# Eleven pairs of projection stripes by seven half-size products instead of eight, and a recurrence taken block by block

## The chip, the cores and the metric

The kernel runs on one core of a Trainium2 chip. The metric is the device time of one launch in microseconds (us); lower is better.

## The reference

One layer of a decoder trunk in fp32, for a prompt of 1024 tokens and 8 single new tokens (1032 columns in all, NT). A normalised input is multiplied by one wide weight; its columns are cut into u and z (recurrent branch and its gate path), q, k, v of 24 heads, za (the gate path of the attention) and two sets of merge gates, g:

```python
D_IN = 2 * D_RNN + 3 * N_GROUPS * D_ATTN + D_ATTN + 2 * D_MODEL      # 9216 columns, D_MODEL = 1024 rows
xn = rms_norm(x, norm_pre);  u, z, q, k, v, za, g_a, g_r = split(xn @ w_in)
xc = causal_conv(u, ...)                          # 4 taps, per channel
r, i = sigmoid(block_diag(xc, w_a) + b_a), sigmoid(block_diag(xc, w_x) + b_x)
a = exp(-8 r softplus(-lam));  b = sqrt(1 - a*a) * i * xc;   h[t] = a[t] h[t-1] + b[t]
y_rnn = (h * silu(z)) @ w_rnn_out
y_att = (merge of three dilated attentions * silu(za)) @ w_attn_out
y = x + rms_norm((sigmoid(g_a) * y_att + sigmoid(g_r) * y_rnn) @ w_out)
```

The new k and v rows, the last convolution inputs and the last h are outputs too.

## The kernel before, in words

Activations lie transposed: 128 channels on the partitions, the 1032 columns (tokens) along the free axis. Eight tiles of the normalised input, each as two fp32r parts (`xh`, `xl`), stay in SBUF as the moving operand. An fp32 product is three fp32r matmuls (`mm3`: hi*hi, hi*lo, lo*hi). A **stripe** is 128 output columns of `w_in`: its 512 KB of weights are loaded by SP, split into `whi` (ACT, L236) and `wlo` (DVE, L237, two instructions of 128x512 each), and multiplied chunk by chunk of the 1032 columns, 8 k-tiles of 3 matmuls each into one PSUM bank. `CHUNKS` cuts the columns into 256, 384 and 392; `EARLY` into 256, 256, 256 and 264. So a stripe is 72 matmuls, or 96 with `EARLY`.

There are 72 stripes. Four (`FIRST`, with `EARLY`) run while the input is still being normalised, up to 72.4 us of the trace. Then come 23 (`EARLY_BLOCKS`: z, u, gates g, za), each evacuated from PSUM as it is made: u by ACT into an `ext` tile, z and za by a sigmoid on ACT and a product on DVE (L563), gates by a sigmoid on ACT (L1131) and a write to DRAM. Beside them runs the recurrence, `chain(j)`, two blocks of 128 channels at a time: convolution on DVE (L587 to L592), splits (L601), 12 small gate matmuls on PE, products on POOL (L619, L649, L659), factors on DVE (L643 to L647) and the scan (L653). The last `chain` falls into the next stage: 36 stripes of q, k and v with the attention beside them. Then come 9 late gate stripes, and from 1065 us the output products.

The program is one stream of matmuls in order. A counter, `clk`, is advanced by `mm`; every other piece of work is a generator in a lane (`spawn`), or a call put off by `later`, and `tick` lets it emit its instructions when `clk` has passed the delay that it yielded. Those delays (`yield 4000` and so on) and the place of `W.work()`, which emits a weight split ahead of its use, set the order of each engine's queue, and each engine then takes its queue strictly in order. Tiles come from an arena of 45 slots of [128 x 1040] fp32 (`new`, `ar.free`).

## Time and profile before

| | us |
|---|---|
| median of 3 runs (1265.29 to 1268.86) | 1267.33 |
| the profiled execution | 1264.49 |
| its span | 1262.7 |
| PE busy in it | 1242.1 |
| DVE, ACT, POOL busy | 607.2, 558.1, 217.3 |

The profiled execution lies 2.84 us under the median, and its span 1.8 us under its own time. Busy time is an engine's time in instructions; a wait in its queue isn't counted.

### The profile page before, as it was taken

How to read it: one execution, taken by the hardware profiler on the slowest of the kernel's cores; microseconds unless marked ns; L12 is line 12 of the kernel's file. 1: busy time of each engine (PE TensorE's matmuls, PEld its weight loads, DVE VectorE, ACT ScalarE, POOL GpSimd, SP SyncE). 2: the span in 40 equal slices, each digit the busy share in tenths (PEclk: the TensorE clock that was granted, in tenths of full speed). 3: DMA queues.
4: the chain of work that ended last, by engine and by line, in shares of the span. 5: the costliest groups of instructions: out<-in, count | busy, mean ns of one | idle time of the engine just before them, and what ended most of it. 6: DMA issues, size and time to landing. Idle time of an engine off the chain costs nothing.

```text
span 1262.7 us, 21509 instructions
## 1 busy us (share of the span) xinstructions
PE 1242.1 (98%) x8701; PEld 1197.0 (95%) x8701; DVE 607.2 (48%) x1319; ACT 558.1 (44%) x1236; POOL 217.3 (17%) x232
## 2 busy tenths in 40 slices
PE   9999999999999999999999999999999999999997
PEld 8999999999988999999998999899999999999997
DVE  6562471582764453644256234644254335554226
ACT  7636646547449844334434344344462322223222
POOL 5000320221300221340026001430027000002001
PEclk9999999999999999999999999999999999999999
DMA  8121223132220144722093124712095375313015
GB/s 258 34 84 51 68 84 89 29 101 67 79 73 5 51 122 102 187 68 50 19 233 90 34 68 116 186 55 68 9 260 152 127 256 168 106 51 118 19 51 201
DMA packets 169929, 125.98 MB, mean 100 GB/s; under 512 B 36009, under 2 KB 155785, under 8 KB 169822
## 3 DMA queue, kind: packets, MB, share of 16 engines
q1 hardware_dynamic: 169830, 124.61, 34.0%
q8 instruction: 68, 1.11, 0.4%
q14 instruction: 31, 0.25, 0.1%
HBM read 98.44 MB, written 26.21 MB: 99 GB/s over the span
## 4 chain that ended last, share of the span: by engine, by line
PE 60%; issue 6%; DVE 3%; ACT 1%; DMA 1%; POOL 1%; SPq 0%; DVEq 0%; ACTq 0%; POOLq 0%
PE ps_pj L157 41%; PE ps_pt L157 10%; PE ps_s L157 3%; PE ps_o L157 3%; PE ps_pt L161 2%; PE ps_s L161 1%; DVE ck L1079 1%; DMA sgd<-sg 1%; DVE wlo L237 1%; POOL uc L619 0%; DVE P L841 0%; ACT P L845 0%; SPq L957 0%; ACT L1131 0%; POOL ck L1076 0%
## 5 line engine op out<-in xcount | busy, mean ns | idle before, releaser
L157 PE MATMUL ps_pj<-xh,whi 128*128 128x256 f32 (+2 forms) x1400 | 457.3, 327 | 2.7 <-DVE vt L736 1.4
L157 PE MATMUL ps_pj<-xh,wlo 128*128 128x256 f32 (+2 forms) x1400 | 445.0, 318 | 0.3 <-DVE wlo L250 0.3
L157 PE MATMUL ps_pj<-xl,whi 128*128 128x256 f32 (+2 forms) x1400 | 445.0, 318 | 0.0
L237 DVE TENSOR_TENSOR wlo<-wraw,whi 128x512 fp32r<-128x512 f32 x176 | 147.2, 839 | 337.6 <-ACT whi L236 326.6
L157 PEld LDWEIGHTS ps_pj<-xh,whi 128*128 128x128 f32 x1400 | 263.2, 188 | 12.2 <-issue 8.2
L157 PEld LDWEIGHTS ps_pj<-xh,wlo 128*128 128x128 f32 x1400 | 263.2, 188 | 0.5 <-DVE wlo L250 0.5
L157 PEld LDWEIGHTS ps_pj<-xl,whi 128*128 128x128 f32 x1400 | 263.4, 188 | 0.1
L845 ACT ACTIVATE P<-P,stat 128x128 f32<-128x128 f32 (+1 forms) x192 | 84.3, 440 | 66.6 <-DVE stat L841 66.6
L157 PE MATMUL ps_pt<-xh,whi 128*128 128x256 f32 (+3 forms) x360 | 112.9, 314 | 0.0
L157 PE MATMUL ps_pt<-xl,whi 128*128 128x256 f32 (+3 forms) x360 | 112.4, 312 | 0.0
L157 PE MATMUL ps_pt<-xh,wlo 128*128 128x256 f32 (+3 forms) x360 | 112.2, 312 | 0.0
L236 ACT ACTIVATE whi<-wraw 128x512 fp32r<-128x512 f32 x176 | 109.7, 625 | 3.7 <-DVE hzl L1264 3.0
L157 PEld LDWEIGHTS ps_pt<-xl,whi 128*128 128x128 f32 x360 | 67.7, 188 | 0.1
L157 PEld LDWEIGHTS ps_pt<-xh,whi 128*128 128x128 f32 x360 | 67.7, 188 | 0.0
L157 PEld LDWEIGHTS ps_pt<-xh,wlo 128*128 128x128 f32 x360 | 67.7, 188 | 0.0
L728 ACT ACTIVATE qt<-ps_pj,qsc 128x384 f32<-128x384 f32 (+1 forms) x36 | 27.6, 767 | 75.7 <-PE ps_pj L157 74.0
L841 DVE CUSTOM_DVE_ANT_0 P<-ps_s,base 128x128 f32<-128x128 f32 (+1 forms) x192 | 56.0, 347 | 7.7 <-PE ps_s L157 6.9
L614 ACT ACTIVATE gate<-ps_s,par 64x256 f32<-64x256 f32 (+2 forms) x96 | 52.1, 543 | 16.9 <-PE ps_s L157 15.6
L862 ACT ACTIVATE PT<-ps_pt 128x256 f32<-128x256 f32 (+1 forms) x48 | 20.9, 435 | 68.0 <-PE ps_pt L161 67.9
L619 POOL TENSOR_TENSOR uc<-uc,gate 128x1032 f32<-128x1032 f32 x8 | 20.2, 2536 | 173.7 <-ACT gate L614 173.7
L732 ACT ACTIVATE kt<-ps_pj 128x384 f32<-128x384 f32 (+1 forms) x36 | 24.4, 677 | 52.0 <-PE ps_pj L157 52.0
L1028 POOL TENSOR_TENSOR ck<-ck,qb 128x1024 f32<-128x1024 f32 x12 | 29.4, 2448 | 104.0 <-DMA ck<-in_cache_kv_w 49.9
(284 smaller groups left out, 2122.8 us busy)
## 6 DMA issues: line engine op xcount, KB each, us to landing
wraw<-in_w_in SPq DMA_DIRECT2D x72, 512.0 KB
ck<-in_cache_kv_w SPq DMA_DIRECT2D x24, 512.0 KB
sgd<-sg SPq DMA_DIRECT2D x16, 516.0 KB
sgl<-sgd SPq DMA_DIRECT2D x16, 516.0 KB
xin<-in_x_prompt SPq DMA_DIRECT2D x16, 512.0 KB
qb<-sd SPq DMA_DIRECT2D x12, 512.0 KB
fb<-fd SPq DMA_DIRECT2D x24, 256.0 KB
hzd<-uc SPq DMA_DIRECT2D x8, 516.0 KB
```

The costliest lines, as they stand in the source:

```text
L157: nc.tensor.matmul(out, lhsT, rhs, start=start, stop=stop)
L161: nc.tensor.transpose(out, in_, idn)
L236: nc.scalar.activation(hi[:, a:b], raw[:, a:b], AF.Copy)
L237: nc.vector.tensor_tensor(lo[:, a:b], raw[:, a:b], f32(hi[:, a:b]), op=OP.subtract)
L614: nc.scalar.activation(G[gate][rows, cs], p[at:at + 64, :n], AF.Sigmoid, bias=par[rows, b, 5 + gate:6 + gate])
L619: nc.gpsimd.tensor_tensor(x, x, gi, op=OP.mult)
L728: nc.scalar.activation(dst, src, AF.Copy, scale=C["qsc"][:, g, hp:hp + 1])
L732: nc.scalar.activation(dst, src, AF.Copy)
L841: nc.vector.tensor_tensor_reduce(out=pt[:, h, :128 * n], in0=ps[h][:, off:off + 128 * n], in1=base, scale=-SLOPES[g][2 * hp + h] * DIL[g], ...
L845: nc.scalar.activation(pt[:, h, :128 * n], pt[:, h, :128 * n], AF.Exp, scale=-1.0, bias=st[:, g, 0, h, b:b + 1], accum_out=st[:, g, 1, h, ...
L862: nc.scalar.activation(t, src, AF.Copy)
L1028: nc.gpsimd.tensor_tensor(kc, kc, qb, op=OP.mult)
```

## The change

The first stage now makes six single stripes (`FIRST` gains z0 and z1). The other 22 stripes ahead of the attention are taken as 11 **pairs** of 256 columns. Weight (8 k-tiles by 2 stripes) and input (8 k-tiles by 1032 columns) are each cut into four quarters, and the four quarters of the output come from seven products of sums of quarters (`STEPS`) where plain blocks take eight. One product is 4 k-tiles, 128 columns of weight and half of the columns (520, in chunks of 256 and 264): 24 matmuls, so a pair has 168.

- Input: the tiles are now kept as two halves of 520 columns with both parts, `X[h, k]`. `make_sums` builds the sums s1, s2 and s4 (three POOL and seven DVE operations for each of four k, three of ACT), `make_s3` builds s3 (one POOL, three DVE, one ACT). The quarter x21 is given up after that, kept in DRAM (`xd`) and split anew by `x21_back` while the last pair runs.
- Weights: `pair_pieces` makes three sums and one more on POOL (L295 to L301), and seven splits (ACT L286, DVE L287), at most `OPS` = 4 operands alive.
- Outputs: DVE adds the products from PSUM into quarters (`add`, L636, 14 a pair) and ACT copies the first (2 a pair). u, z, za and g go to DRAM (`leave`).
- Recurrence: `lru(b)` takes one block at a time in five reserved slots, reads u and z back from DRAM and makes z's silu itself (ACT, and one more product on POOL, L902). It runs beside the pairs and the attention. The silu of za moved into the merge behind the attention.
- All single stripes now use `EARLY`; there are 6 + 36 + 8 of them. The PSUM banks are given out by stage (`MODES`).

```diff
-LATE_GATES = 9
-FIRST = [("u", 0), ("u", 1), ("g", 0), ("g", 1)]
-EARLY_BLOCKS = [("z", 0), ("z", 1), ("u", 2), ("u", 3), ("g", 2), ("g", 3),
-                ("z", 2), ("z", 3), ("u", 4), ("u", 5), ("g", 4), ("g", 5),
-                ("z", 4), ("z", 5), ("u", 6), ("u", 7), ("g", 6), ("a", 0),
-                ("z", 6), ("z", 7), ("a", 1), ("a", 2), ("a", 3)]
+LATE_GATES = 8
+FIRST = [("u", 0), ("u", 1), ("g", 0), ("g", 1), ("z", 0), ("z", 1)]
+PAIRS = [("u", 2), ("g", 2), ("z", 2), ("u", 4), ("g", 4), ("z", 4), ("u", 6), ("g", 6), ("z", 6), ("a", 0), ("a", 2)]
...
+        def pair_pieces(self, i):
+            r0, r1 = self.raw[i]
...
+                self.live += 1
+                return t
+            def split(name, src):
+                t = op(name)
+                nc.scalar.activation(t[:, 0], src, AF.Copy)
+                nc.vector.tensor_tensor(t[:, 1], src, f32(t[:, 0]), op=OP.subtract)
...
+            def first():
+                split("b11", b11)
+                t.append(new([128, 2, 4, 128], F32, "wsum"))
+                t1, t2 = t[0][:, 0], t[0][:, 1]
+                nc.gpsimd.tensor_tensor(t1, b12, b11, op=OP.subtract)
+                nc.gpsimd.tensor_tensor(t2, b22, t1, op=OP.subtract)
+                nc.gpsimd.tensor_tensor(b12, b22, b12, op=OP.subtract)
+            def second():
+                split("t2", t[0][:, 1])
+                nc.gpsimd.tensor_tensor(t[0][:, 1], b21, t[0][:, 1], op=OP.subtract)
+            def third():
+                split("t3", b12)
+                ar.free(r0)
+            def sixth():
+                split("t4", t[0][:, 1])
+                ar.free(t[0])
```

```diff
+    def make_sums():
+        for k in range(4):
+            x11, x12, x21, x22 = X[0, k], X[0, k + 4], X[1, k], X[1, k + 4]
+            s1, s2, s4 = (SX.setdefault((q, k), new([128, 2, HALF], F32R, q)) for q in ("s1", "s2", "s4"))
+            ta, tb = (new([128, 2, HALF], F32, "xsum") for _ in range(2))
+            nc.gpsimd.tensor_tensor(ta[:, 0], f32(x21[:, 0]), f32(x21[:, 1]), op=OP.add)
+            nc.vector.tensor_tensor(ta[:, 1], f32(x22[:, 0]), f32(x22[:, 1]), op=OP.add)
+            nc.sync.dma_start(xd[k], ta[:, 0])
+            nc.gpsimd.tensor_tensor(tb[:, 1], f32(x12[:, 0]), f32(x12[:, 1]), op=OP.add)
+            nc.vector.tensor_tensor(tb[:, 0], f32(x11[:, 0]), f32(x11[:, 1]), op=OP.add)
+            yield 1200
+            nc.gpsimd.tensor_tensor(ta[:, 1], ta[:, 0], ta[:, 1], op=OP.add)
+            nc.vector.tensor_tensor(tb[:, 0], ta[:, 1], tb[:, 0], op=OP.subtract)
+            nc.vector.tensor_tensor(tb[:, 1], tb[:, 1], tb[:, 0], op=OP.subtract)
+            yield 1200
+            both = ((s1, ta[:, 1]), (s2, tb[:, 0]), (s4, tb[:, 1]))
+            for t, src in both:
+                nc.scalar.activation(t[:, 0], src, AF.Copy)
+            yield 1000
+            for t, src in both:
+                nc.vector.tensor_tensor(t[:, 1], src, f32(t[:, 0]), op=OP.subtract)
+            ar.free(ta, tb)
+            yield 1200
...
+    def make_s3():
+        for k in range(4):
+            while len(ar.slots) < 3:
+                yield 500
+            x11, x21 = X[0, k], X.pop((1, k))
+            t = new([128, 2, HALF], F32, "xsum")
+            s3 = SX["s3", k] = new([128, 2, HALF], F32R, "s3")
+            nc.gpsimd.tensor_tensor(t[:, 0], f32(x21[:, 0]), f32(x21[:, 1]), op=OP.add)
+            nc.vector.tensor_tensor(t[:, 1], f32(x11[:, 0]), f32(x11[:, 1]), op=OP.add)
+            ar.free(x21)
+            yield 600
+            nc.vector.tensor_tensor(t[:, 1], t[:, 1], t[:, 0], op=OP.subtract)
+            nc.scalar.activation(s3[:, 0], t[:, 1], AF.Copy)
+            nc.vector.tensor_tensor(s3[:, 1], t[:, 1], f32(s3[:, 0]), op=OP.subtract)
+            ar.free(t)
```

```diff
+    def x21_back():
+        for k in range(0, 4, 2):
+            while len(ar.slots) < 4:
+                yield 500
+            t = new([128, 2, HALF], F32, "xsum")
+            nc.sync.dma_start(t, xd[k:k + 2].rearrange("k p c -> p k c"))
+            yield 3500
+            for q in range(2):
+                x = X[1, k + q] = new([128, 2, HALF], F32R, "x1b")
+                nc.scalar.activation(x[:, 0], t[:, q], AF.Copy)
+                nc.vector.tensor_tensor(x[:, 1], t[:, q], f32(x[:, 0]), op=OP.subtract)
+            ar.free(t)
...
+    STEPS = (("b11", "x11"), ("t2", "s2"), ("t3", "s3"), ("t1", "s1"), ("b21", "x12"), ("t4", "x22"), ("b22", "s4"))
...
+    def project_pair(close, last=False):
+        i = W.use_pair()
+        p1 = [small.tile([128, 264], F32, tag="t1", name="p1") for _ in range(2)]
+        for step, (wname, xname) in enumerate(STEPS):
+            w = W.op(i, wname)
+            if step == 1:
+                tb = new([128, 2, HALF], F32, "qb")
+            if step == 3:
+                ta = new([128, 2, HALF], F32, "qa")
+            for c, (o, n) in enumerate(((0, 256), (256, 264))):
+                p = ps_tile("c")[:, :n]
+                for k in range(4):
+                    x = x_op(xname, k)
+                    mm3(p, w[:, 0, k], w[:, 1, k], x[:, 0, o:o + n], x[:, 1, o:o + n], k == 0, k == 3)
+                    if k == 1:
+                        W.work()
+                        yield None
+                cs = slice(o, o + n)
+                q1, q2 = tb[:, 0, cs] if step else None, tb[:, 1, cs] if step else None
+                add = lambda to, by: nc.vector.tensor_tensor(to, p, by, op=OP.add)
+                if step == 0:
+                    nc.scalar.activation(p1[c][:, :n], p, AF.Copy)
+                elif step == 1:
+                    add(q2, p1[c][:, :n])
+                elif step == 2:
+                    add(q1, q2)
+                elif step == 3:
+                    add(q2, q2)
+                    add(ta[:, 1, cs], q1)
+                elif step == 4:
+                    add(ta[:, 0, cs], p1[c][:, :n])
+                elif step == 5:
+                    add(q1, q1)
+                else:
+                    add(q2, q2)
+                yield None
+            W.drop(i, wname)
...
+                    ar.free(SX.pop(("s1", k)))
+                spawn("sums", x21_back())
```

```diff
+    def lru(b):
...
+        L = room["L"]
+        e, r, x = L(0, [128, EXT]), L(1, [128, CV]), L(2, [128, NT])
...
+        s, z = L(0, [128, NT]), L(1, [128, NT])
+        nc.sync.dma_start(z, zd[b])
...
+        nc.scalar.activation(a, z, AF.Sigmoid)
+        yield 3500
+        nc.gpsimd.tensor_tensor(z, z, a, op=OP.mult)
+        nc.gpsimd.tensor_tensor(x, x, z, op=OP.mult)
```

```diff
     for e in started:
         advance(e)
+    spawn("sums", make_sums())
+    for what, i in FIRST[4:]:
+        advance(proj_uz(what, i))
+    until(lambda: "sums" not in lanes)
+    mode[0] = "pair"
+    spawn("sums", make_s3())
     clear_low_w()
-    C = late_consts()
...
+    def lru_start():
+        while "sums" in lanes or len(ar.slots) < 7:
+            yield 500
+        room["L"] = Room(ar, 5)
+    spawn("lru", lru_start())
+    for b in range(KB):
+        spawn("lru", lru(b))
...
+    for q, (what, i) in enumerate(PAIRS):
+        advance(project_pair(pair_of(what, i), last=q == len(PAIRS) - 1))
```

**Ahead of the first pair, DVE and POOL.** DVE before, from the first weight split (of the fifth stripe) after the four first stripes; `cv`, `uc` and `low_w` are the recurrence's, `zs` the silu of z:

```order
L237 TENSOR_TENSOR wlo_1087<-wraw_381,whi_1086 128x512
L582 TENSOR_TENSOR low_w_135<-lrw_850,lh 64x128 x2
L587 SCALAR_TENSOR_TENSOR cv_1110<-ext_269,par,cv_1110 128x1056
L588 SCALAR_TENSOR_TENSOR cv_1110<-ext_269,par,cv_1110 128x1056
L563 TENSOR_TENSOR zs_1085<-ps_pt,zs_1085 128x256
L237 TENSOR_TENSOR wlo_1087<-wraw_381,whi_1086 128x512
L563 TENSOR_TENSOR zs_1085<-ps_pj,zs_1085 128x384
```

DVE of the change from the split of z1's weights; `x` are input tiles, `xsum` the plain sums, `s` the sums' parts:

```order
L268 TENSOR_TENSOR wlo_972<-wraw_390,whi_971 128x512
L560 TENSOR_TENSOR xsum_995<-x_4_29_128 128x520
L563 TENSOR_TENSOR xsum_996<-x_0_17_116 128x520
L566 TENSOR_TENSOR xsum_996<-xsum_995,xsum_996 128x520
L567 TENSOR_TENSOR xsum_996<-xsum_996 128x520
L268 TENSOR_TENSOR wlo_972<-wraw_390,whi_971 128x512
L574 TENSOR_TENSOR s_64_992<-xsum_995,s_64_992 128x520
L574 TENSOR_TENSOR s_65_993<-xsum_996,s_65_993 128x520
L574 TENSOR_TENSOR s_66_994<-xsum_996,s_66_994 128x520
L560 TENSOR_TENSOR xsum_1069<-x_5_30_129 128x520
L563 TENSOR_TENSOR xsum_1070<-x_1_18_117 128x520
```

POOL of the change at the same place; the program before has no such sums:

```order
L559 TENSOR_TENSOR xsum_995<-x_0_25_124 128x520
L562 TENSOR_TENSOR xsum_996<-x_4_21_120 128x520
L565 TENSOR_TENSOR xsum_995<-xsum_995 128x520
L559 TENSOR_TENSOR xsum_1069<-x_1_26_125 128x520
L562 TENSOR_TENSOR xsum_1070<-x_5_22_121 128x520
L565 TENSOR_TENSOR xsum_1069<-xsum_1069 128x520
L295 TENSOR_TENSOR wsum_1145<-wraw_421 128x512
```

DVE goes on in that manner to the last part of s3, L592. From the first row shown to that one it has 49 rows; 47 of them take two tiles from SBUF, and two take one of theirs from PSUM. POOL has 20 sums up to there, and two clears of `low_w`. In the old program POOL's next sum of two tiles comes only with L619.

**A pair, DVE and POOL.** DVE before, in the recurrence's second half:

```order
L643 SCALAR_TENSOR_TENSOR gate_1369<-gate_1368,gate_1369 128x1032
L645 TENSOR_SCALAR gate_1368<-gate_1369 128x1032
L237 TENSOR_TENSOR wlo_1737<-wraw_1536,whi_1736 128x512
L647 SCALAR_TENSOR_TENSOR sq_1690<-gate_1368,sq_1690 128x1032
L563 TENSOR_TENSOR zs_1735<-ps_pj,zs_1735 128x256
L643 SCALAR_TENSOR_TENSOR gate_1389<-gate_1388,gate_1389 128x1032
L237 TENSOR_TENSOR wlo_1737<-wraw_1536,whi_1736 128x512
L645 TENSOR_SCALAR gate_1388<-gate_1389 128x1032
L563 TENSOR_TENSOR zs_1735<-ps_pt,zs_1735 128x384
L647 SCALAR_TENSOR_TENSOR sq_1692<-gate_1388,sq_1692 128x1032
L563 TENSOR_TENSOR zs_1735<-ps_pt,zs_1735 128x392
```

DVE of the change, in the fourth pair; `wop` are a pair's weight operands, `qa` and `qb` the quarters, `room` the recurrence's tiles:

```order
L287 TENSOR_TENSOR wop_2487<-wraw_2241,wop_2487 128x512
L636 TENSOR_TENSOR qb_2271<-ps_c,qb_2271 128x256
L636 TENSOR_TENSOR qb_2271<-ps_c,qb_2271 128x264
L287 TENSOR_TENSOR wop_2528<-wsum_2438,wop_2528 128x512
L287 TENSOR_TENSOR wop_2566<-wraw_2242,wop_2566 128x512
L636 TENSOR_TENSOR qb_2558<-ps_c,p_2515 128x256
L888 SCALAR_TENSOR_TENSOR room_2310<-room_2309,room_2310 128x1032
L636 TENSOR_TENSOR qb_2558<-ps_c,p_2516 128x264
L890 TENSOR_SCALAR room_2310<-room_2310 128x1032
L287 TENSOR_TENSOR wop_2599<-wsum_2438,wop_2599 128x512
L636 TENSOR_TENSOR qb_2558<-ps_c,qb_2558 128x256
L892 SCALAR_TENSOR_TENSOR room_2491<-room_2310,room_2491 128x1032
```

POOL of the change at that place:

```order
L295 TENSOR_TENSOR wsum_2438<-wraw_2241 128x512
L296 TENSOR_TENSOR wsum_2438<-wraw_2242,wsum_2438 128x512
L297 TENSOR_TENSOR wraw_2241<-wraw_2242,wraw_2241 128x4x128
L808 COPY us<-qa_2346 128x8
L301 TENSOR_TENSOR wsum_2438<-wraw_2242,wsum_2438 128x512
L878 TENSOR_TENSOR room_2132<-room_2132,room_2310 128x1032
L808 COPY us<-qb_2271 128x8
L894 TENSOR_TENSOR room_2491<-room_2491,room_2132 128x1032
L899 COPY cst<-room_2132 128x9
L902 TENSOR_TENSOR room_2492<-room_2492,room_2309 128x1032
L903 TENSOR_TENSOR room_2132<-room_2132,room_2492 128x1032
```

The additions from PSUM, the splits of the next operands and the recurrence now stand in one DVE queue, and the weight sums stand in POOL's queue among the recurrence's products.

## Rows read from the trace of the kernel before

**Rows 1.** The page: busy time of each engine, and the granted TensorE clock in 40 slices.
```profile
PE 1242.1 (98%) x8701; PEld 1197.0 (95%) x8701; DVE 607.2 (48%) x1319; ACT 558.1 (44%) x1236; POOL 217.3 (17%) x232
...
PEclk9999999999999999999999999999999999999999
```
**Rows 2.** Windows: stretch, length, PE PEld DVE ACT POOL busy (instructions), PEclk, DMA share, GB/s.
```profile
72.40:349.50 277.10, 277.10 (x1767) 277.10 (x1766) 143.96 (x169) 153.14 (x251) 53.77 (x51) 1.00 0.25 74
349.50:500.00 150.50, 145.68 (x1023) 136.60 (x1022) 74.32 (x176) 89.92 (x194) 16.44 (x9) 1.00 0.22 60
...
1065.00:1155.50 90.50, 90.50 (x577) 90.50 (x576) 48.62 (x89) 20.15 (x40) 1.02 (x4) 1.00 0.29 88
```
**Rows 3.** The chain that ended last, output stage: start us, length us, engine, tile, line, matmuls.
```profile
1147.05 8.51 PE ps_pj L157 x48
1155.56 5.65 PE ps_pt L157 x48
```
**Rows 4.** Timeline of PE at 72.4 us: start us, length us, instruction.
```profile
72.46 0.28 PE L157 MATMUL ps_pt<-xh,whi 128*128 128x256 f32 x1
```
**Rows 5.** Timeline of ACT, the same place; in brackets idle time and its releaser.
```profile
72.66 0.39 ACT L1131 ACTIVATE sg<-ps_pt 128x264 f32<-128x264 f32 x1 [2.53 <-PE ps_pt L157]
72.95 0.63 ACT L236 ACTIVATE whi<-wraw 128x512 fp32r<-128x512 f32 x1
```
**Rows 6.** Timeline of DVE, the same place.
```profile
73.61 0.69 DVE L237 TENSOR_TENSOR wlo<-wraw,whi 128x512 fp32r<-128x512 f32 x1 [5.66 <-ACT whi L236]
```
**Rows 7.** Single lines: count, then shortest/median/longest in ns, first and last start, forms.
```profile
L237 DVE TENSOR_TENSOR wlo<-wraw,whi x176: 669/692/2892, 28.1 to 1217.0; 128x512 fp32r<-128x512 f32 x176
...
L587 DVE SCALAR_TENSOR_TENSOR cv<-ext,par,cv x8: 1317/1318/1321, 75.1 to 354.2; 128x1056 f32<-128x1056 f32 x8
...
L601 DVE TENSOR_TENSOR uc<-uc,uc x16: 1227/1228/1230, 87.6 to 369.1; 64x1032 fp32r<-64x1032 f32 x16
...
L619 POOL TENSOR_TENSOR uc<-uc,gate x8: 2416/2423/2884, 125.7 to 416.9; 128x1032 f32<-128x1032 f32 x8
...
L647 DVE SCALAR_TENSOR_TENSOR sq<-gate,sq x8: 1214/1226/1234, 146.6 to 441.9; 128x1032 f32<-128x1032 f32 x8
...
L653 DVE TENSOR_TENSOR_SCAN gate<-gate,sq x8: 2260/2280/4504, 156.8 to 453.9; 128x1024 f32<-128x1024 f32 x8
```
**Rows 8.** Timeline of POOL, 147 to 163 us.
```profile
147.94 2.42 POOL L649 TENSOR_TENSOR sq<-sq,uc 128x1032 f32<-128x1032 f32 x1 [17.02 <-DVE sq L647]
154.40 2.42 POOL L649 TENSOR_TENSOR sq<-sq,uc 128x1032 f32<-128x1032 f32 x1 [4.04 <-DVE sq L647]
...
159.97 2.41 POOL L659 TENSOR_TENSOR uc<-gate,zs 128x1032 f32<-128x1032 f32 x1
```
**Rows 9.** Timeline of DVE, 147 to 163 us.
```profile
148.05 3.40 DVE L643 SCALAR_TENSOR_TENSOR gate<-gate,gate 128x1032 f32<-128x1032 f32 x1
...
156.30 0.57 DVE L563 TENSOR_TENSOR zs<-ps_pt,zs 128x392 f32<-128x392 f32 x1 [2.03 <-ACT zs L562]
...
160.21 2.72 DVE L237 TENSOR_TENSOR wlo<-wraw,whi 128x512 fp32r<-128x512 f32 x1
```
**Rows 10.** Groups by form: count | busy us, mean ns of one | idle before, releaser.
```profile
L563 DVE TENSOR_TENSOR zs<-ps_pt,zs 128x256 f32<-128x256 f32 x4 | 1.7, 421 | 5.3 <-ACT zs L562 5.3
...
L572 POOL TENSOR_SCALAR low_w<-ident 128x128 fp32r<-128x128 f32 x4 | 2.2, 579 | 0.0
```
**Rows 11.** Windows after PE's last matmul, columns as in rows 2.
```profile
1254.00:1256.00 2.00, 0.00 (x0) 0.00 (x0) 1.61 (x5) 1.01 (x3) 0.57 (x2) 1.00 1.02 382
1256.00:1258.00 2.00, 0.00 (x0) 0.00 (x0) 1.39 (x8) 0.28 (x2) 1.06 (x1) 0.64 0.42 160
1258.00:1260.00 2.00, 0.00 (x0) 0.00 (x0) 1.46 (x3) 0.00 (x0) 0.00 (x0) 0.50 0.45 173
```
**Rows 12.** The chain that ended last, a transfer in it.
```profile
954.40 7.12 DMA sgd<-sg
```

More of the change, by code (lines that the diff above doesn't have):

```diff
@@ L567, in hybrid_step, with spill @@
-    low_w = [const.tile([128, 256], F32R, name=f"low_w{i}") for i in range(2)]
+            nc.scalar.activation(t[:, c0:c0 + n], p[:, :n], AF.Copy)
+        yield from project(evac)
+        def spill():
+            if what == "u":
+                nc.gpsimd.tensor_copy(us[:, b], t[:, SEQ:])
+                nc.sync.dma_start(ud[b], t[:, :SEQ])
+            else:
+                nc.sync.dma_start(zd[b], t)
+            ar.free(t)
+            kept_uz.add((what, b))
+        later(1000, spill)
@@ L569, in clear_low_w @@
+    low_w = [const.tile([128, 256], F32R, name=f"low_w{i}") for i in range(1)]
     def clear_low_w():
@@ L1131, in evac @@
             nc.scalar.activation(z[:, c0:c0 + n], p[:, :n], AF.Sigmoid)
-        yield from project(evac, chunks)
+        yield from project(evac)
         def spill():
```

381 lines of the change are left out of this document (223 added, 158 removed).

## The prediction

> **What bounds the kernel now.** I read the busy times first. PE works 1242.1 us of a span of 1262.7 and its granted clock is 9 in all 40 slices [rows 1], so the kernel is a stream of matmuls with hardly a gap, and a change gains by giving PE fewer columns and loses by making PE wait. Then I read the windows [rows 2]. In the stretch of the 23 early stripes, 72.4 to 349.5 us, PE has no idle time, DVE is busy 144 of 277 us and POOL 54. In the stretch after it, where the last two recurrence blocks run beside the attention, PE loses 150.50 - 145.68 = 4.8 us. The chain of waits gives the price of a matmul at full clock: 48 of 256 columns take 5.65 us, 117.7 ns each, and 48 of 384 and 392 take 8.51 [rows 3]. Eight stripes take the 90.5 us of the last window [rows 2], 11.31 us each; 24 of their 72 matmuls have 256 columns (2.82 us), so the other 48 take 176.8 ns at a mean of 388. A column is then (176.8 - 117.7) / 132 = 0.448 ns, a matmul of 264 columns 121.3 ns, and a stripe in four chunks 72 x 117.7 + 24 x 121.3 ns = 11.39 us.
>
> **The sum is made against the profiled execution, 1264.49 us; the median of the runs is 2.84 us above it, which I add at the end.**
>
> **A. Seven products for eight: -27.9 us.** A pair is 168 matmuls, half of 256 and half of 264 columns: 84 x (117.7 + 121.3) ns = 20.08 us. Two stripes were 22.62. Eleven times 2.54 is 27.9 us off PE.
>
> **B. Four chunks for three in the other stripes: +3.4.** 46 stripes (z0, z1, 36 of q, k, v, 8 gates) go from 11.31 to 11.39 us.
>
> **C. The sums ahead of the first pair: +28 (4 to 33).** In the trace the first matmul after the four first stripes starts at 72.46 [rows 4]. In the change z0 and z1 run from there, 2 x 11.39, to 95.2, then the first product, which needs no sum (2.87 us), the second, and at some 102 us PE wants s3, whose last part is the last of DVE's row of sums. When can DVE have it? Its sums stand behind z1's first weight split. That split waits for ACT's half, which stands behind the evacuation of the last gate stripe: here 72.66 and 72.95 [rows 5], and the corresponding DVE split starts at 73.61 [rows 6]. From there to the last of s3 DVE has 47 operations on two SBUF tiles of 512 or 520 columns. A split of 512 takes 0.692 us [rows 7], so I take 0.70, together 32.9 us. POOL has 20 sums; two may be done by then, and 18 remain at 2.423 x 520/1032 = 1.22 us [rows 7], with two clears of 0.58 [rows 10]: 23.1 us.
>
> These two do not run beside each other. At 147.94 POOL starts a product of 2.42 us; DVE's L643 starts 0.11 us later and takes 3.40 us where L647, of the same shape, takes 1.226 [rows 7 to 9]: it stood still until POOL was done (147.94 + 2.42 + 1.23 = 151.6; it ends at 151.45). The same at 159.97: DVE's split, 0.24 us later, takes 2.72 in place of 0.69 [rows 8, 9]. But at 156.30, with POOL busy from 154.40 to 156.82, DVE's L563, whose one input is in PSUM, takes its usual 0.57 [rows 8, 9]. So two inputs from SBUF on DVE and a sum on POOL exclude each other; one input from PSUM does not. The Trainium skill, *SBUF — State Buffer*, section "Who interferes with whom", says the same as a rule: a DVE instruction with two SBUF inputs contends with a GpSimd instruction that reads SBUF, and whoever issued first holds the shared port for the whole instruction. By that rule every sum here takes part, and term C is 28; by the rows alone, which show it for lengths of 512 and 1032 columns in two collisions, the first rival below stays open.
>
> The work of the two engines then adds up: 73.5 + 32.9 + 23.1 = 129.5 us for the last of s3 against 102: +28 with the last hand-over between ACT and DVE. Lower end: no exclusion and no hand-overs, 73.5 + 32.9 = 106.4, +4. Upper end: with an ACT copy and a queue step in each of four rounds not hidden, +33. I take 28, because it is nearest to the two collisions shown.
>
> **D. The clock during that wait: +2 (0 to 6).** Nothing in PE's stream before shows a gap of that length. After PE's last matmul, which ends by 1254, the granted clock is 1.00 to 1256, 0.64 on the mean to 1258 and 0.50 after that [rows 11]: the lower of the two levels, 1.2 for 2.4 GHz. A PE that stands still for 28 us will come back at that level, and its first matmuls take double time until it rises. How soon it rises no row shows; I take 2 us, and 6 if the first two products run at half.
>
> **E. Pairs two to eleven: +11 (0 to 44).** PE has 10 x 20.08 and the gate matmuls of about 4.6 recurrence blocks (12 matmuls, 1.88 us by the prices above): 209 us. DVE has 70 splits (48.4), about 4.5 blocks of recurrence on two SBUF tiles (2 x 1.318 + the same for 1024 columns, 1.28 + 2 x 1.228 + 2 x 1.226 + 2.28 and small ones, 11.5 us [rows 7], together 52), 140 additions from PSUM at 0.421 to 0.43 [rows 10], 60 us, and 3 us of one-input work. POOL has 40 weight sums of 1.20 (48) and four products a block, since the silu of z is now one of them: 4 x 2.42 x 4.4 = 43. If POOL's 91 us lie entirely under additions and idle time, the excluded work is 100 + 91 = 191 us of 209, and nothing is lost. If none does, DVE needs 100 + 60 + 3 + 91 = 254, and PE waits 44. PE can bridge a delay of three operands made ahead (some 8 us) and six PSUM banks of 1.4 us each. But DVE's queue is strict: a blocked split or recurrence step holds up the additions behind it, these hold the banks, and the gate matmuls stand in PE's queue until DVE has made `xs`. With 191 of 209 in the good case there is little room; I take a quarter of the way.
>
> **F. Three and a half recurrence blocks beside the attention, where there were two: +3 (-2 to +10).** The two cost 4.8 us of PE waits at most [rows 2]. The blocks now come singly, so waits can also get less. ACT also changes its table oftener, and its gates, exps and za's silu stand in a queue with the attention's; I take half as much again, plus a little.
>
> **G. x21 back from DRAM: +1 (0 to 5).** Two reads of 520 KB and four splits lie beside the second half of the last pair and the first products of v, some 10 to 16 us. The nearest transfer, a write of 516 KB in the chain, took 7.12 us [rows 12]. Late, it costs PE a few us.
>
> **At nothing:** the writes of u and z and their reloads. SP issues them among the weight loads, whose DMA share in that stretch is 0.25 [rows 2]; they would cost what E costs if a block's reload were late, since the recurrence has no one waiting for it before the rnn output product. The late gates and the output stage keep their order.
>
> Sum: -27.9 + 3.4 + 28 + 2 + 11 + 3 + 1 = +20.5, that is 1285.0 in the profiled execution and **1288 us** against the median.
>
> **The rivals.** *No exclusion among the sums.* DVE and POOL work side by side at 73.5 to 110 us; what is left is DVE's own 32.9 us and its waits for POOL, C about 10, D 0, E 0: -27.9 + 3.4 + 10 + 3 + 1 = -10.5, 1257 us: faster. It decides as soon as C, D and E together stay under 20. For it: 520 columns are shorter than the products of 1032, and DVE could slip between them. Against it: both collisions of rows 9, one of them a split of just 512.
> *Everything hidden*, with the sums begun early enough: C 0 to 1, which leaves 1243, or 1247 with F and G. Against it is the late start at 73.6.
> *Balance.* The exclusion holds but the sums hide partly, C 20, D 1, E 5, F and G 0: +1.5, so 1269, within 0.3%.
> *The pairs run at DVE's pace.* As the forecast, with E at 44: 1321 us. For it: DVE's 163 and POOL's 91 us together exceed PE's 209 in the whole stretch. Against it: the additions, a quarter of that, need not exclude POOL.
> That the change doesn't do what it says I give nothing: the instructions of PE in order show 24 per product and seven products per pair.
>
> **How the numbers follow.** 0.3% (3.8 us) is about what a measurement of this kernel can tell from no change; the same is then 1263.5 to 1271.1. Forecast, 1272 to 1304: 0.50. Pairs at DVE's pace: 0.15. Balance: 0.12. No exclusion: 0.17. Everything hidden: 0.06. So faster 0.23, same 0.12, slower 0.65. The range leaves out "everything hidden" and the far end of the worst case: 1252 to 1316. The likeliest case's own range is 1272 to 1304.
>
> **What would show it.** C: one gap of PE of 20 us or more, between 98 and 131 us, that ends with a part of s2 or s3 on DVE, with DVE and POOL taking turns and their busy times together near the gap's length; D: a granted clock under 1.00 there alone. E: in the pairs, PE waits on L287, on L636's banks or on `xs`, of 5 to 20 us in all, with DVE splits of 1.5 us and more beside POOL's sums. A: 24 matmuls of a product in 2.87 us. The forecast is wrong if PE's gap ahead of the first pair is under 10 us, or if DVE's sums keep 0.70 us beside a busy POOL.

## The result and the profile after

The changed kernel takes 1385.94 us (median of four runs, 1383.51 to 1386.87) against 1267.02 for the kernel before, timed beside it: a ratio of 1.0935 (95% interval 1.0914 to 1.0956), 9.3% slower. The forecast was 1288, with a range up to 1316: the side was right, the size was not. The profiled execution took 1386.87, 122.4 us over the one before.

The page of the changed kernel, engines' busy time and granted clock, beside [rows 1]:

```profile
PE 1270.8 (92%) x10069; PEld 1215.1 (88%) x10069; DVE 743.8 (54%) x1527; ACT 620.1 (45%) x1312; POOL 344.7 (25%) x326
...
PEclk9996998988999999996999999999999999999999
```

PE is busy 92% of the span, and the clock, 9 in every slice before, has dips: two slices of 6 and three of 8 (a slice is 35 us, so each is a mean over stretches at the full and at the lower level, 2.4 and 1.2 GHz). PE's busy time is 29 us longer although it has fewer columns to do. The windows say where; first two of the kernel before, up to the first scores of the attention and up to the first output product (columns as in rows 2):

```profile
72.40:384.80 312.40, 309.72 (x1968) 308.86 (x1967) 162.48 (x192) 169.32 (x279) 53.77 (x51) 1.00 0.24 72
384.80:1019.50 634.70, 629.15 (x4502) 589.29 (x4502) 288.97 (x779) 280.50 (x714) 133.44 (x60) 1.00 0.38 100
```

and the changed kernel, by stages: z0 and z1 (z0 starts at 71.2, 1.3 us earlier than the stripe at that place did before); the wait for the sums; the pairs; the first q, k, v; the rest up to the first output product; the output.

```profile
72.40:98.70 26.30, 21.78 (x184) 21.57 (x182) 22.61 (x24) 9.87 (x21) 17.02 (x11) 0.99 0.41 140
98.70:126.10 27.40, 13.33 (x58) 10.95 (x58) 23.12 (x27) 6.83 (x13) 13.88 (x13) 0.62 0.15 53
126.10:416.50 290.40, 249.93 (x1859) 244.20 (x1860) 199.72 (x304) 140.77 (x213) 117.19 (x158) 0.91 0.30 99
416.50:453.10 36.60, 35.12 (x296) 34.81 (x294) 19.41 (x29) 16.05 (x27) 8.96 (x10) 1.00 0.45 134
453.10:1142.00 688.90, 647.04 (x5435) 604.19 (x5435) 326.15 (x813) 337.65 (x797) 161.79 (x81) 0.96 0.36 95
1142.00:1385.10 243.10, 234.27 (x1698) 233.15 (x1696) 116.11 (x234) 63.73 (x157) 12.51 (x28) 0.99 0.37 125
```

Up to the first scores the change takes 380.7 us where 312.4 went before, +68.3; from there to the output 688.9 for 634.7, +54.2, with one stripe less; the output stage is the same. So the loss is in two places, and the second is one that the prediction had priced at 3 us.

**The wait for the sums.** PE's timeline (start, length, in brackets idle time and its releaser):

```profile
98.73 2.93 PE L176 MATMUL ps_c<-x,wop 128*128 128x256 f32 x12 [4.55 <-ACT z L783]
108.18 3.01 PE L176 MATMUL ps_c<-x,wop 128*128 128x264 f32 x12 [6.52 <-ACT z L783]
...
118.87 0.58 PE L176 MATMUL ps_c<-s,wop 128*128 128x256 f32 x1 [2.50 <-ACT s L591]
...
125.39 0.58 PE L176 MATMUL ps_c<-s,wop 128*128 128x256 f32 x1 [1.43 <-ACT s L591]
126.12 7.53 PE L176 MATMUL ps_c<-s,wop 128*128 128x256 f32 x38 [0.15 <-DVE s L592]
```

PE gets the last part of s3 (L592) at 126.1. Without a wait it would have wanted it at about 101: z1 ends at 94.2, and 58 matmuls of 119.5 ns follow. So the wait costs 25 us. It is not one gap: PE stands still for 4.55 and 6.52 us behind the evacuation of z, then for 2.50, 2.02 and 1.43 us between the parts of s3, and works at a mean clock of 0.62 in between. The 38 matmuls after it take 7.53 us for some 4.5 at full clock, since the granted clock is 0.50 until 132: 3 us more. DVE and POOL take turns over the sums:

```profile
75.46 1.80 DVE L566 TENSOR_TENSOR xsum<-xsum,xsum 128x520 f32<-128x520 f32 x1 [1.21 <-POOL xsum L565]
77.30 1.70 DVE L567 TENSOR_TENSOR xsum<-xsum 128x520 f32<-128x520 f32 x1
...
95.51 0.70 DVE L566 TENSOR_TENSOR xsum<-xsum,xsum 128x520 f32<-128x520 f32 x1 [1.17 <-POOL xsum L565]
```

```profile
75.39 1.32 POOL L559 TENSOR_TENSOR xsum<-x 128x520 f32<-128x520 f32 x1
76.66 1.78 POOL L562 TENSOR_TENSOR xsum<-x 128x520 f32<-128x520 f32 x1
```

A sum of 520 columns that takes DVE 0.70 us with POOL idle (at 95.51) takes 1.80 and 1.70 beside a POOL sum. That is what the Trainium skill, *SBUF — State Buffer*, "Who interferes with whom", says of two SBUF inputs on DVE; these rows agree, at a length at which the trace before had none.

**The pairs.** PE's longest groups of waits there (us in total, times, longest):

```profile
PE ps_s L176 <- DVE room L863: 16.0, 5, 4.1
PE ps_c L176 <- DVE qb L636: 10.4, 5, 4.2
PE ps_c L176 <- DVE wop L287: 7.4, 7, 2.6
PE ps_c L176 <- ACT wop L286: 4.2, 3, 2.6
```

With the shorter groups they are 40.5 us in all. Two of them followed back, by the timelines of ACT, DVE, POOL and PE:

```profile
265.57 0.42 ACT L843 ACTIVATE lh<-lw 128x256 fp32r<-128x256 f32 x1 [3.07 <-DMA lw<-in_lru_w_x]
267.87 1.27 ACT L847 ACTIVATE room<-room,par 128x1056 f32<-128x1056 f32 x1 [1.89 <-DMA room<-ud]
269.05 0.62 ACT L286 ACTIVATE wop<-wsum 128x512 fp32r<-128x512 f32 x1
```

```profile
266.02 0.61 DVE L846 TENSOR_TENSOR low_w<-lw,lh 64x128 fp32r<-64x128 f32 x2 [2.46 <-ACT lh L843]
...
269.77 0.69 DVE L287 TENSOR_TENSOR wop<-wsum,wop 128x512 fp32r<-128x512 f32 x1 [2.68 <-ACT wop L286]
...
271.72 2.20 DVE L850 SCALAR_TENSOR_TENSOR room<-room,par,room 128x1056 f32<-128x1056 f32 x1
273.85 0.75 DVE L636 TENSOR_TENSOR qb<-ps_c,qb 128x256 f32<-128x256 f32 x2
...
276.19 1.63 DVE L852 SCALAR_TENSOR_TENSOR room<-room,par,room 128x1024 f32<-128x1024 f32 x1
...
279.18 2.49 DVE L863 TENSOR_TENSOR room<-room,room 64x1032 fp32r<-64x1032 f32 x2 [0.53 <-ACT room L862]
```

```profile
270.54 2.27 POOL L295 TENSOR_TENSOR wsum<-wraw 128x512 f32<-128x512 f32 x1 [2.38 <-DVE wop L287]
```

```profile
274.40 2.02 PE L176 MATMUL ps_c<-x,wop 128*128 128x256 f32 x12 [4.17 <-DVE qb L636]
280.55 0.55 PE L176 MATMUL ps_s<-room,lh 128*128 128x256 f32 x1 [4.12 <-DVE room L863]
```

The gate weights of a recurrence block come late from DRAM. ACT stands still for them (3.07 us) and for u (1.89); the split of the next operand (L286), which waits for neither, stands behind them in ACT's queue. DVE stands still for both in turn (2.46 and 2.68). Then the convolution (L849 to L852, one of them 2.20 beside POOL's weight sum) stands ahead of two additions from PSUM (273.85), PE's bank comes free 4.17 us late, and 2 us further on the gate matmuls, put into PE's queue for a time at which x should have been split, wait 4.12 us for L863. No engine is overloaded in this: each has idle time in the same 16 us.

**Beside the attention.** The largest wait of the run, in PE, DVE and POOL:

```profile
643.89 3.57 PE L176 MATMUL ps_s<-one,ck 128*128 128x1 f32 x16 [15.92 <-DVE ck L1310]
```

```profile
631.80 1.23 DVE L888 SCALAR_TENSOR_TENSOR room<-room,room 128x1032 f32<-128x1032 f32 x1 [8.62 <-ACT room L886]
...
638.42 4.01 DVE L896 TENSOR_TENSOR_SCAN room<-room,room 128x1024 f32<-128x1024 f32 x1 [1.15 <-POOL room L894]
...
642.61 1.22 DVE L1310 TENSOR_TENSOR ck<-ck,ck 128x1024 f32<-128x1024 f32 x1
651.02 0.69 DVE L996 COPY vn<-ps_s 128x512 f32<-128x512 f32 x1 [7.19 <-POOL zal L1191]
```

```profile
635.20 3.19 POOL L894 TENSOR_TENSOR room<-room,room 128x1032 f32<-128x1032 f32 x1 [5.68 <-DVE room L892]
638.36 1.93 POOL L1307 TENSOR_TENSOR ck<-ck,pT 128x1024 f32<-128x1024 f32 x1
...
643.85 2.37 POOL L902 TENSOR_TENSOR room<-room,room 128x1032 f32<-128x1032 f32 x1
646.30 2.37 POOL L903 TENSOR_TENSOR room<-room,room 128x1032 f32<-128x1032 f32 x1
648.62 2.37 POOL L1191 TENSOR_TENSOR zal<-zal,szl 128x1024 f32<-128x1024 f32 x1
```

The last recurrence block meets the first sample and the first merge. DVE stands 8.62 us for ACT's part of the block (L886). POOL's product L894 waits 5.68 us for DVE (L892), and the sample's product (L1307) stands behind it in POOL's queue. The scan waits for L894, takes 4.01 us beside L1307, and holds the sample's sum (L1310) behind it. PE waits 15.92 us for that sum, and then DVE's copy of v waits 7.19 us for the silu of za, last in POOL's queue.

### The profile page after: what moved, and what is told of

The parts are those of the page before. It is cut to its first block, busy times and chain, and to the rows that moved or that the text cites. A ratio compares the mean times of both kernels' runs of the same rounds, so it can differ in the third digit from the quotient of the medians.

```text
span 1385.1 us, 25005 instructions
## 1 busy us (share of the span) xinstructions
PE 1270.8 (92%) x10069; PEld 1215.1 (88%) x10069; DVE 743.8 (54%) x1527; ACT 620.1 (45%) x1312; POOL 344.7 (25%) x326
## 5 line engine op out<-in xcount | busy, mean ns | idle before, releaser
L176 PE MATMUL ps_pj<-x,whi 128*128 128x256 f32 (+1 forms) x2496 | 469.5, 288 | 2.6 <-ACT kt L957 2.0
L176 PEld LDWEIGHTS ps_pj<-x,whi 128*128 128x128 f32 x2496 | 388.4, 191 | 11.5 <-issue 6.3
L176 PE MATMUL ps_pj<-x,wlo 128*128 128x256 f32 (+1 forms) x1248 | 353.5, 283 | 0.2 <-DVE wlo L331 0.2
L176 PEld LDWEIGHTS ps_pj<-x,wlo 128*128 128x128 f32 x1248 | 237.5, 190 | 0.4 <-DVE wlo L331 0.4
L176 PE MATMUL ps_c<-s,wop 128*128 128x264 f32 (+1 forms) x1056 | 149.7, 300 | 17.3 <-ACT s L591 6.7
L176 PEld LDWEIGHTS ps_c<-s,wop 128*128 128x128 f32 x1056 | 143.5, 205 | 21.5 <-ACT s L591 7.7
L176 PE MATMUL ps_pj<-x1b,whi 128*128 128x264 f32 (+1 forms) x704 | 134.9, 289 | 5.0 <-ACT qt L953 2.7
L176 PE MATMUL ps_c<-x,wop 128*128 128x264 f32 (+1 forms) x792 | 110.2, 296 | 25.7 <-ACT z L783 11.1
L176 PEld LDWEIGHTS ps_c<-x,wop 128*128 128x128 f32 x792 | 104.8, 200 | 28.7 <-ACT z L783 11.6
L176 PEld LDWEIGHTS ps_pj<-x1b,whi 128*128 128x128 f32 x704 | 110.3, 192 | 6.6 <-ACT qt L953 2.9
L287 DVE TENSOR_TENSOR wop<-wraw,wop 128x512 fp32r<-128x512 f32 x44 | 53.7, 1221 | 35.0 <-ACT wop L286 34.9
```

The costliest lines, as they stand in the source:

```text
L176: nc.tensor.matmul(out, lhsT, rhs, start=start, stop=stop)
L287: nc.vector.tensor_tensor(t[:, 1], src, f32(t[:, 0]), op=OP.subtract)
```

## The experiments

All are the changed kernel with an edit, or with the edits of an earlier one and one or two more. Times are medians, of two runs each (x3: three). Ratios, with 95% intervals in brackets, are against the kernel before, timed beside each group; its median lay between 1266.95 and 1269.70, so times of different groups (x1 to x4, x5 to x8, x9 to x12, x13 to x15, the change) compare to some 3 us.

**1. The recurrence without pairs (x1).** Each pair becomes two single stripes, and no input sums are made.

```diff
...
-        advance(project_pair(pair_of(what, i), last=q == len(PAIRS) - 1))
+        for r in range(2):
+            advance(proj_g(*GATES[i + r]) if what == "g" else proj_uz(what, i + r))
```

> The changed kernel with each pair taken as two single stripes (no sums, no seven products); the block-by-block recurrence, its reloads, the four chunks and the PSUM banks' modes stay, with the wide banks in the first stages. za is kept plain as in the change. Theory 1 (the pairs and the sums load DVE and POOL, which exclude each other, and the recurrence suffers with them): the stretch ahead of the attention has under 5 us of PE waits and a clock of 1.00, the recurrence gets further before the attention, and the whole takes 1268 to 1290 us. Theory 2 (the recurrence in five slots, one block at a time, is itself what PE waits for): PE still waits 10 us and more on the line of the xs split ahead of the attention, 30 and more beside it, and the time stays above 1310.

1332.53 us, ratio 1.050 (1.039 to 1.062). Neither theory had it whole: ahead of the attention PE waits under 7 us, near theory 1's 5, and the time stays above 1310, as theory 2 said, since most of the loss beside the attention is there:

```profile
402.00:1081.60 679.60, 639.82 (x5432) 599.54 (x5432) 325.57 (x810) 331.98 (x791) 161.55 (x81) 0.97 0.36 96
```

That stage takes 679.6 us for 688.9 in the change and 634.7 before. So most of the loss beside the attention needs no pairs.

**2. The pairs without recurrence (x3).**

```diff
-        L = room["L"]
...
-        nc.gpsimd.tensor_tensor(x, x, z, op=OP.mult)
+        x = room["L"](2, [128, NT])
+        nc.sync.dma_start(x[:, :SEQ], ud[b])
+        nc.gpsimd.tensor_copy(x[:, SEQ:], us[:, b])
```

> The changed kernel without the recurrence: u is only carried from its place to that of the result, so the convolution, gates, scan and silu of z are left out (and 96 gate matmuls, 15 us of PE). Theory 1: the pairs alone have 4.8 us of splits, 4.8 of POOL and 6 of additions in 20.1 us, which fits; from 126 us on the ten and a half pairs take 213 to 225 us, the attention's stretch loses its 36 us of waits and the total is 1245 to 1270. A rival (the pairs' own chain of sums, splits and additions is too slow by itself): the pairs still take 240 us and more, and the total stays above 1280.

1257.43 us, ratio 0.990 (0.987 to 0.993), in the range of theory 1.

```profile
129.00:347.50 218.50, 218.34 (x1802) 218.27 (x1802) 121.26 (x244) 58.46 (x103) 66.60 (x130) 0.99 0.41 136
```

From the sums on, the 74.5 products left are 214 us at 2.87, and PE waits only 0.2 us. The window takes 218.5 us because its ends hold a few matmuls more and its first 5 us lie at a clock of 0.50; from 137 to 347 us, 1753 matmuls take 210.0 us, 119.8 ns each for the 119.5 of the prediction. The pairs' own splits, weight sums and additions fit beside PE. This shows that the seven products give what they should and that the loss in the pairs comes with the recurrence.

It shows a limit too. This run leaves out 15 us of gate matmuls and is only 12 us faster than the kernel before. An estimate from these two numbers: even with a recurrence that costs PE no wait, the change would gain nothing, since the wait for the sums takes what the seven products save.

**3. A faster lane (x8).** Every delay of `lru(b)` times 0.6 (`yield 3000` becomes `yield 1800`, and so on).

> The changed kernel with every delay of the recurrence's lane times 0.6, nothing else: its instructions are given out earlier, about 40 us a block in place of 60, so that it ends before the first sample's and merge's products. Theory 1 (the 58 us lost beside the attention come from the last three and a half blocks meeting the attention, the sample and the merge on POOL and DVE): PE's waits from 417 us on fall from 36 to under 12 with no low clock at 620 to 660, worth 30 to 50 us, and the pairs lose 10 to 30 more since their DVE and POOL are fuller: 1350 to 1390. Rival (the attention is slow for its own new shape, four chunks a stripe, the tables, za's silu in the merge): the loss there stays at 45 us or more and the total rises.

1451.06 us, ratio 1.145 (1.141 to 1.148). Half of theory 1's expectation came true, half failed badly:

```profile
126.10:536.00 409.90, 271.41 (x1890) 264.96 (x1891) 254.75 (x349) 192.22 (x275) 149.68 (x186) 0.81 0.25 83
...
572.70:1205.80 633.10, 626.74 (x5391) 589.32 (x5391) 288.07 (x774) 266.39 (x716) 129.91 (x56) 0.99 0.36 96
```

```profile
PE ps_s L176 <- DVE room L863: 106.0, 8, 17.9
```

With the recurrence over before the attention, that stage takes 633.1 us for 688.9 (631.6 in x3). But the pairs take 410 us for 290, 106 of them gate matmuls that wait for x; ACT stands 64.7 us for gate weights (L843), 18.8 in the change. This speaks for lateness in queues that go strictly in order, but it doesn't exclude load: all eight blocks now stand beside the pairs, where there were five. DVE is busy 55 us more in a stretch that is 120 us longer.

**4 to 7. Load taken away or moved.** The four weight sums left out (x2); the 16 input sums on DVE (x4); the recurrence's four products on DVE (x6); the input sums, the weight sums, these products and za's silu on DVE (x5). One line of each of the first three:

```diff
...
-                nc.gpsimd.tensor_tensor(t1, b12, b11, op=OP.subtract)
...
-            nc.gpsimd.tensor_tensor(ta[:, 0], f32(x21[:, 0]), f32(x21[:, 1]), op=OP.add)
+            nc.vector.tensor_tensor(ta[:, 0], f32(x21[:, 0]), f32(x21[:, 1]), op=OP.add)
...
-        nc.gpsimd.tensor_tensor(s, s, x, op=OP.mult)
+        nc.vector.tensor_tensor(s, s, x, op=OP.mult)
```

> The changed kernel without the four weight sums of each pair on POOL; the operands are split from plain quarters, so this part of the computation is left out, the number of splits, matmuls and additions is the same. It takes 11 x 4.8 = 53 us off POOL and nothing off DVE. Theory 1 (exclusion): the stretch of the pairs, 291 us in the change from 126 to 417, loses a third or more of its 69 us over the plain matmul time, PE's waits there fall from 40 to under 25, and the total falls by 25 to 60 us, to 1325 to 1360. Theory 2 (only the queue order and the recurrence's lateness): under 10 us.

1365.91 us (ratio 1.076, 1.073 to 1.080): 20 us, between the theories; PE's waits in the pairs fall from 40.5 to 28.9 us.

> The changed kernel with the sixteen input sums of POOL ahead of the first pair done by DVE. Theory 1 (DVE and POOL take turns, so their times add): 16 sums of 1.22 become 16 of 0.70, the wait for s3 ends 6 to 10 us earlier than 126.1, at 116 to 120, and the total falls by 4 to 10 us. Rival (they run side by side, and DVE's own row of 33 us is what takes the time): the wait ends 5 to 11 us later, at 131 to 137, and the total rises by as much.

1382.01 us (1.089, 1.085 to 1.093). The last part of s3 comes at 117.6 for 126.1, as theory 1 had it, and against the rival. Some of it may be the four hand-overs from POOL's sum to DVE's (1.17 to 1.21 us each in the change), which x4 takes away too; the turns themselves show in the rows above. Of the 8.5 us about half is left at the end.

> The changed kernel with only the recurrence's four products a block on DVE, the weight sums left on POOL. Theory 1: shared time falls by 4 x (2.42 - 1.23) = 4.8 us a block, 38 us over the eight, and the products no longer stand in one POOL queue with weight sums, sample and merge: total down by 15 to 45 us. Rival (queue order and lateness): within 10 us of 1386.

1377.29 us (1.086, 1.083 to 1.090): 9 us, just inside the rival's 10.

> The changed kernel with all of POOL's new sums and products on DVE: the input sums, the four weight sums of a pair, the four products of a recurrence block and the silu of za. POOL keeps the sample's and the merge's own products. Theory 1 (in the pairs DVE and POOL take turns, so a POOL operation of 1.2 or 2.4 us costs DVE its full length): DVE gets 40 sums of 0.69 and some 18 products of 1.23 in the pairs where POOL took 48 and 43 us, so the shared time falls by 40 us, PE's waits in the pairs fall from 40 to 10 to 25 and the total by 25 to 60, to 1325 to 1360. Rival (they run side by side enough, and what PE waits for is the order and lateness of DVE's queue): DVE's queue only gets longer by 50 us, and the total stays or rises, 1380 to 1420.

1373.24 us (1.083, 1.077 to 1.089): 13 us. POOL's busy time from the first pair on falls from 131 to 17 us, and PE's waits behind the sums only from 40.5 to 37.8. The total lies between the theories. Theory 1 falls as the main account of the pairs: the taking of turns is real, but ending it leaves PE's waits nearly as they were; that DVE is longer busy for it (204.8 for 198.8 us) is part of this run. In x2 the operands also no longer stand behind POOL's queue, and the two can't be told apart there.

**8. More cover for the sums (x7).** `FIRST` gets g2 and g3, and ten pairs are left.

> The changed kernel with the gates g2 and g3 as single stripes behind z1, so ten pairs, and 22.8 us more of plain matmuls over the input sums. Theory 1 (the wait ahead of the first pair is the sums' own 56 us from 73.5 on): s3 is still ready at about 126, PE now wants it at 125, so the wait and its low clock (24 us together) nearly vanish, less 2.5 us for the pair given up: total down by 15 to 22 us, to 1364 to 1371. Rival (the sums are stretched by whatever work runs beside them): down by under 8 us.

1356.39 us (1.070, 1.067 to 1.073): 30 us, more than expected. The sums' last part is ready at 133.9, and the waits for it fall to some 4 us. That is 20 us; the rest is a pair less with the recurrence beside it, or chance of the order, which no run tells apart.

**9 to 12. Order.** The reloads of the next block ahead, with u's ahead of the gate weights (x9), then three longer delays, two of which are shown (x10), then x7's and x5's edits on top (x11, x12).

```diff
...
         nc.scalar.activation(a, z, AF.Sigmoid)
+        if ("u", b + 1) in kept_uz:
+            yield from fetch(b + 1)
...
-        yield 1500
+        yield 4000
         xs = [L(q, [128, NT], F32R) for q in range(2)]
...
-        yield 3000
+        yield 7000
         for q in range(2):
             rows = slice(64 * q, 64 * q + 64)
```

> The changed kernel with the next block's u and gate weights read back right after the scan of the block before, 8.5 us of the planner's time earlier, in the same slot; nothing else is moved. Theory 3 (formed after the first eight runs: the heads of ACT's and DVE's queues stand still for the reloads, 18.8 us for the gate weights and 7.6 for u in the pairs, and the splits and additions behind them come late): the waits of L843 on the gate weights vanish but for a block or two, PE's gaps in the pairs fall from 54 to 35 to 45, the total by 15 to 40 us. Theory 1 (the shared time of DVE and POOL): no change beyond 8 us, since no work is taken away.

1359.6 us (1.072, 1.062 to 1.083). The total is in theory 3's range and the reason is not: ACT still waits 25.3 us for the gate weights in the pairs (two waits; why these reloads still came late was not followed), and PE's waits in the pairs are 36.8 us. So the run doesn't try what it was meant to try. The gain is beside the attention, where the recurrence now ends earlier (last scan at 581 for 638).

> The kernel of x9 with three delays of the recurrence's lane longer: 2500 for 1000 ahead of the first DVE taps, 4000 for 1500 ahead of ACT's copies of x, 7000 for 3000 ahead of the gate matmuls (the old chain had 7500 there). Theory 3: PE's 16 us of waits on the xs split (L863) fall under 4, ACT's 20 us on L853 under 6, the pairs' gaps to 15 to 30, but each block takes 8 us more, so more of the recurrence stands beside the attention: total 5 to 25 us under x9. Theory 1: within 8 us of x9, or slower by the later recurrence.

1346.99 us (1.062, 1.050 to 1.075): 13 us under x9, in theory 3's range.

```profile
126.10:381.00 254.90, 235.03 (x1848) 230.89 (x1849) 199.66 (x301) 131.98 (x197) 117.14 (x157) 0.97 0.33 110
```

PE's waits on the split of x fall from 14.1 to 0.3 us, all its waits in the pairs to 19.9, and the pairs' stretch from 290 to 255. DVE's and POOL's work in it is the same (199.66 and 117.14 us for 199.72 and 117.19); of the gate matmuls, four blocks' stand in it for five (1.9 us). No load was taken away; three delays were made longer, and which of them counts isn't told apart. Two things limit this. ACT's waits for x (L853 in the change) were to fall from 20 to under 6 us and stayed at 19.0. And of the 34 us that the stretch loses against x9 only 13 are left at the end: the last scan is now at 648, and from the pairs' end on x10 takes 21 us longer than x9.

> The kernel of x10 with g2 and g3 as single stripes ahead of the pairs, as in x7. If the wait for the sums and the recurrence's lateness are separate losses, the gain of x7 (30 us) comes on top: 22 to 32 us under x10, 1290 to 1330.

1336.34 us (1.054, 1.045 to 1.063): 11 us, half of what was expected. PE's waits for the sums fall to under 5 us, and the recurrence stands a little longer beside the attention (last scan at 654).

> The kernel of x11 with all of POOL's new sums and products on DVE, as in x5. Theory 1 would have a further 20 to 50 us here; theory 3 gives 5 to 15, as in x5 (13 us), mostly from the input sums.

1331.45 us (1.050, 1.039 to 1.062): 5 us, at the lower end of theory 3's.

**13 to 15. Beside the attention.** The first sample waits until the recurrence is done (x13, on x10); then the same with x12's edits (x14); then nine pairs (x15).

```diff
     def sample(hp):
+        while "lru" in lanes:
+            yield 1000
```

> The kernel of x10 with the first sample's generator held until the recurrence's lane is empty; no operation is added or left out. If the loss beside the attention (55 us against a run without the recurrence there) is the meeting of the last blocks with the first sample's products, PE's gaps of 11.5 and 3.9 us at 599 to 606 and the low clock behind them go, and the total falls by 15 to 30 us, to 1317 to 1332. Rival (the merge's eight POOL products and the attention itself are enough): under 8 us.

1322.58 us (1.044, 1.040 to 1.048): 24 us under x10.

```profile
422.10:1076.90 654.80, 634.97 (x5436) 596.81 (x5436) 321.55 (x818) 338.29 (x799) 161.39 (x81) 0.99 0.38 102
```

From the first scores to the output 654.8 us for 678.5 in x10 and 688.9 in the change: against the run without a recurrence (631.6 us in x3, and 5.7 for the gate matmuls) x10 loses 41 us there and x13 17, so the meeting with the first sample is the larger part of the loss.

> The kernel of x12 (ten pairs, two more singles, all new sums on DVE) with the first sample held as in x13. By the first account 15 to 30 us under x12, 1301 to 1316; by the rival within 8 us of 1331.

1303.48 us (1.029, 1.025 to 1.033): 28 us under x12. The stretch is 645.4 us, 12 over the run whose recurrence was over, of which 6 are gate matmuls. Between the pairs and the first scores it takes 52.9 us for the change's 36.6, with two waits of PE of 7.2 and 4.8 us; no run followed these.

> The kernel of x14 with g4 and g5 as single stripes too, so nine pairs, and the last delay of a recurrence block 2000 for 5000. If what is left of the pairs' loss is crowding on DVE's queue, 22.8 us more of plain stripes, in which the recurrence can run, are worth more than the 2.5 us that the pair saved: 3 to 15 us under x14. If the pairs run free by now, 2.5 us over x14.

1305.14 us (1.030, 1.026 to 1.035), not told apart from x14. Both were slower than the kernel before, as every version with the recurrence was.

## Why the prediction was wrong

| term | forecast | measured |
|---|---|---|
| A, seven products | -27.9 | about -27.4 (x3: 119.8 ns a matmul) |
| B, four chunks | +3.4 | as forecast for z0 and z1 (11.40 us each), the rest not measured alone |
| C, the sums | +28 (4 to 33) | about +25 (126.1 - 101) |
| D, their clock | +2 (0 to 6) | about +3 (38 matmuls in 7.53 us) |
| E, the pairs | +11 (0 to 44) | about +63 |
| F, beside the attention | +3 (-2 to +10) | about +59 |
| G, x21 | +1 | at most +1 (36.6 us for three stripes, 35.3 before) |

For E: 290.4 us less 214 for the products, 9.4 for five blocks' gate matmuls, 3 of D and 1 of the next stripe. For F: 54.2 us longer, with a stripe less (11.3), and with four chunks (3.3) and 1.7 blocks' gate matmuls (3.1) more.

**A, C and D held, size and mechanism.** DVE's and POOL's sums were to be ready at 129.5 if their times add up; they are at 126.1. The sign asked for one gap of 20 us, and it is several (above). One detail was not foreseen: PE first waits for a bank that z's evacuation holds, since ACT's queue has copies of the sums ahead of it (4.55 and 6.52 us, "ACT z L783").

**E failed in its price.** The prediction names the mechanism: a blocked split or recurrence step holds up the additions behind it, and the gate matmuls stand in PE's queue until DVE has made `xs`. But it set the price by adding up work, 191 or 254 us of DVE and POOL against 209 of PE, and took a quarter of the way to 44; measured are some 63, above its own upper end. Experiment 2 shows that the pairs alone leave PE no wait. How much is load and how much is order shows in the stretch from s3's last part to the pairs' last matmul: 289.5 us in the change, 271.8 without the weight sums (x2), 281.0 with POOL's new work on DVE (x5), 254.0 with longer delays and DVE's and POOL's work unchanged (x10). So load has a part, and lateness more, about half of E; the clock's share lies in both.

Two steps of the prediction passed this by. Under "At nothing" it put the reloads, "since the recurrence has no one waiting for it before the rnn output product". Nothing waits for the recurrence's result, but its instructions that wait stand in ACT's, DVE's and PE's queues with weight splits, PSUM additions and products behind them, as the rows at 265 to 281 us show; what the late reloads alone cost is not shown, since x9 didn't remove their waits and left the stretch at 288.2 us. And the delay ahead of the gate matmuls had gone from `yield 7500` to `yield 3000`, which the kernels show and the prediction didn't weigh; x10, which gives most of it back and lengthens two others, brings PE's waits on the split of x from 14.1 to 0.3 us.

**The clock was priced at one place only.** In the pairs the granted clock is 0.91 over 290.4 us, worth some 26 us; 3 of them follow the wait for the sums (D), so the 40 us of waits cost some 63. The prediction expected a clock under 1.00 at the first wait alone. PE was busy without a gap from 126 to 145 us, and the clock was back at 1.00; then it waits 2.84 us for L863, up to 148, and the next window lies at 0.72:

```profile
140.00:147.00 7.00, 5.14 (x43) 4.92 (x42) 6.97 (x11) 2.67 (x4) 1.87 (x2) 1.00 0.30 112
147.00:153.00 6.00, 5.02 (x28) 5.02 (x29) 4.13 (x6) 3.27 (x8) 0.00 (x0) 0.72 0.11 44
153.00:160.00 7.00, 7.00 (x58) 7.00 (x58) 3.00 (x7) 5.50 (x10) 0.00 (x0) 1.00 0.04 8
```

The Trainium skill, *TensorE: Matmul & The Clock Gate*, section "HAM oscillation — how this bites in real kernels", tells of a kernel in which a wait that comes back in every round brings the lower clock back each time. These windows agree, and so does the mean of 0.91. The prediction had a row for the fall itself [rows 11] and applied it to the first wait alone.

**F failed by place.** It scaled the old wait (4.8 us for two blocks, [rows 2]) by the number of blocks, +3 us. The price goes with what they meet more than with their number: in the kernel before, the last scan is at 453.9, ahead of the first sample; in the change it is at 638, among the first sample's and the first merge's products. x8 (recurrence over: 633.1) shows that the loss comes with the recurrence's presence there, and x13 (sample held: 24 us under x10) that the meeting with the first sample is over half of it. What makes up the other 17 us in x13 is open.

The rival "no exclusion" is out by the first wait. The rival "pairs at DVE's pace", 1321 us, had the pairs' price (44 us) nearer than the forecast had, but with DVE's load as the reason, and with no loss of this size beside the attention. What stays open: how the waits left in the pairs (20 us in x10) divide between load and lateness, which of x10's three delays counts, and whether the copy of v waits for za's silu because it takes over its slot, which the releaser suggests and no run tried alone.
